# The mixing norms' sums of squares: two 512-column products with a matrix of ones, and each partition's token read from the diagonals

## The chip, the cores and the metric

The kernel runs on one core of one Trainium2 chip. The metric is the device time of one execution in microseconds (us), the median of three runs. Engines are named as in the profile: PE is TensorE's matmul stream, DVE is VectorE, ACT is ScalarE, POOL is GpSimd, SP is the engine that issues most DMAs.

## What is computed

Two layers of an encoder trunk on 512 tokens of 1024 channels. Both halves of a layer begin with an RMS norm: the mixing half (gates, a convolution, three kinds of attention) and the feed-forward half.

```python
def _rmsnorm(x, g):
    xf = x.astype(jnp.float32)
    y = xf * lax.rsqrt(jnp.mean(jnp.square(xf), axis=-1, keepdims=True) + EPS)
    return (y * g.astype(jnp.float32)).astype(x.dtype)

for l in range(DEPTH):
    h = _rmsnorm(x, g_mix[l])
    proj = h @ w_in[l]
    ...
    x = x + mixed @ w_out[l]
    x = x + _conv_ffn(_rmsnorm(x, g_ffn[l]), w_up[l], ...)
```

The kernel multiplies by the gain at once and by the reciprocal root only behind the products, since it is one number per token.

## The kernel before, in words

The stream x lies channel-major: eight tiles of 128 channels by 512 tokens. `norm_tile` (L290 on) writes each tile's gain-scaled copy as two parts that add up to it (`xh`, `xl`, type fp32r) and adds its squares into `sqacc`, 128 by 512, so that the sum over partitions is still to be made. Weights come in units of 128 by 1024: an SP DMA into `w_raw` (L218, two buffers), ACT's high part `w_hi` (L222) and DVE's low part `w_lo` (L224), three buffers each. Every product is then three fp32r matmuls (high by high, low by high, high by low).

Token-major projections (`token_major`, L467 to L469) put 128 tokens on the partitions and 512 output columns in each of four PSUM banks; there the norm is one number per partition, `rstd[:, b]`. Each layer begins with two of them: queries and keys of the neighbourhood attention, into the four banks named aux, and the values (`project_v`), into the four banks named mm. Other projections are channel-major and need the norm as a row `RB`, the same on all partitions.

`finish_norm` makes both for the two mixing norms. It is a generator in the list `side`; `tick` advances it behind a stretch of products, so PE has its matmuls in the middle of the first token-major projection (layer 1) or at its end (layer 0). It makes four matmuls with 128 columns of `sqacc` as weights and one column of ones as the moving operand (L350), which leaves token p of block b in row p, column b of a bank. DVE reads 128 by 4 (L354), takes the reciprocal root by Newton's steps (`newton`, L272 to L277, eleven small operations), and POOL writes `rstd` to DRAM (L358) and reads it back onto all partitions (L362); ACT puts it in the order of the tokens (`RB`, L366). The feed-forward norms (`broadcast_norm`) do it another way: `sqacc` is split into two fp32r parts (`sqh`, `sql`), and two matmuls with a 128 by 128 matrix of ones (L328) leave every token's sum on all partitions.

What follows `rstd` at a layer's start, in the order of the chain: ACT copies the four aux banks to `Q` times `rstd` (L600) and squares them (L501), DVE sums the squares per head (L502), `rsqrt8` takes the root (L575 to L580, with L515 twelve small operations), DVE scales the four `Q` (L519), and PE transposes them by matmuls with an identity (L537), eight at the first visit. PE's own order is fixed: these eight stand behind 72 matmuls of the values' projection.

The order of the work on each engine is made by a scheduler that goes by dependencies and priorities; `self.first()` and the weights' `high_priority` move work ahead, and a smaller edit can move neighbours.

Of the kernel before, what the change touches and what calls it, by code (L numbers as in the profile page):

```python
# [14 lines left out]
F32 = mybir.dt.float32  # L15
F32R = mybir.dt.float32r
I32 = mybir.dt.int32
AF = mybir.ActivationFunctionType
ALU = mybir.AluOpType
# [3 lines left out]
P = 128  # L23
L = 2
D = 1024
S = 512
KT = D // P
NB = S // P
# [6 lines left out]
EPS = 1e-6  # L35
# [16 lines left out]
C_ID, C_ONE, C_COS, C_SIN, C_DIL, C_SWA = 0, 128, 136, 200, 264, 1160  # L52
# [136 lines left out]
class Trunk:  # L189
# [99 lines left out]
    def norm_tile(self, d, xn, pool, lead=False):  # L289
# [17 lines left out]
        else:  # L307
            sq = pool.tile([P, S], F32, name="sq", tag=self.sq_tag, bufs=2)
            nc.scalar.activation(sq, xn, AF.Square)
            nc.vector.tensor_tensor(self.sqacc, self.sqacc, sq, ALU.add)  # L310

    def broadcast_norm(self):

        nc = self.nc
        v = nc.vector
        sqacc = self.sqacc

        def work():
            tile = lambda n, t, dt: self.fp.tile([P, S], dt, name=n, tag=t, bufs=1)
            one, hi, lo = (tile(n, t, F32R) for n, t in (("one", "e0"), ("sqh", "e1"), ("sql", "e2")))  # L320
            v.memset(one[:, :P].bitcast(F32), 1.0)
            with self.first():
                nc.scalar.activation(hi, sqacc, AF.Copy)
                v.tensor_tensor(lo, sqacc, hi.bitcast(F32), ALU.subtract)
            yield
            ps = self.aux()
            for x in (hi, lo):
                nc.tensor.matmul(ps, lhsT=one[:, :P], rhs=x, start=x is hi, stop=x is lo)  # L328
            ms, q = (tile(n, t, F32) for n, t in (("ms", "e3"), ("rs_q", "e5")))
            self.RB = self.norm.tile([P, S + PHASE], F32, name="RB", tag="RB", bufs=1)[:, :S]  # L330
            with self.first():
                v.tensor_scalar(ms, ps, 1.0 / D, EPS, ALU.mult, ALU.add)
                self.newton(ms, tile("rs_i", "e4", I32), q, self.RB)
            yield

        self.side.append(work())

    def finish_norm(self, delay, later=0, mid=0):

        nc = self.nc  # L340
        sqacc = self.sqacc
        self.rstd = self.norm.tile([P, NB], F32, name="rstd", tag="rstd", bufs=2)
        rstd = self.rstd

        def work():
            for _ in range(delay):
                yield
            ps = self.mm()
            for b in range(NB):
                nc.tensor.matmul(ps[:, b:b + 1], lhsT=sqacc[:, b * P:(b + 1) * P],  # L350
                                 rhs=self.cst[:, C_ONE:C_ONE + 1], start=True, stop=True)
            with self.first():
                v = self.norm.tile([P, NB], F32, name="ms", tag="ms", bufs=2)
                nc.vector.tensor_scalar(v, ps[:, 0:NB], 1.0 / D, EPS, ALU.mult, ALU.add)  # L354
                self.rsqrt(self.norm, v, [P, NB], rstd)

            row = self.dram.tile([S], F32, name="row", tag="row", bufs=2)
            nc.gpsimd.dma_start(row.rearrange("(p b) -> p b", p=P), rstd)  # L358
            for _ in range(mid):
                yield  # L360
            raw = self.scratch()
            nc.gpsimd.dma_start(raw, row.unsqueeze(0).broadcast_to([P, S]))  # L362
            for _ in range(later):
                yield
            self.RB = self.norm.tile([P, S + PHASE], F32, name="RB", tag="RB", bufs=1)[:, :S]
            nc.scalar.activation(self.RB.rearrange("q (b p) -> q b p", b=NB),  # L366
                                 raw.rearrange("q (p b) -> q b p", b=NB), AF.Copy)
            yield

        self.side.append(work())  # L370


# [522 lines left out]
    def ffn(self, l, last):  # L895
# [3 lines left out]
        for i in range(4):  # L899
# [3 lines left out]
            U.append(u)  # L903
        F, self.got = [], {}
        self.load_quad(l, 0)
        for i in range(NF):
# [29 lines left out]
            v.tensor_tensor(fl, f, ys[0], ALU.mult)  # L936
            F.append(fl)
            if i in EARLY:
                self.split_pair(F, EARLY.index(i), self.got)
        return F  # L940

# [67 lines left out]

    def split_pair(self, F, j, got):  # L1010

        nc = self.nc
        v = nc.vector
        fi, fk = F[2 * j:2 * j + 2]

# [199 lines left out]
    def layer(self, l):  # L1215
        tc = self.tc
        last = l == L - 1
        self.Y, self.mixed, self.MH, self.glu_u = [None] * 4, [], [], []
        with tc.tile_pool(name="gate", bufs=1, reuse_waits="tile") as self.gp:
            with tc.tile_pool(name="attn", bufs=1, reuse_waits="tile") as self.ap:  # L1220
                self.scratch = lambda: self.gp.tile([P, S], F32, name="raw", tag="t1", bufs=2)
                pss = self.token_major(None, self.aux) if l == 0 else self.early
                Q = self.new_Q()
                for b in range(NB):
                    self.evac_q(Q)(b, pss[b])
                with self.first():
                    for _ in self.qk_stats(Q, 4, 4, None):
                        pass
                self.derive_params()
                V = self.new_V()  # L1230
                self.tabs = [None] * 4
                self.queue(chain(self.na_biases(l, 3 if l else 5), self.qk_norm(Q, 4, 4, 0),
                                 self.attention('na', V, 1)))
                Vd = self.new_V()
                self.project_v(V, Vd)
                Q = self.project_qk()
                ready = self.beside(self.qk_stats(Q, 4, 4, 0))
                self.queue(chain(ready, self.qk_norm(Q, 4, 4, 2), self.attention('dil', Vd, 2)))
                self.glu()
                self.side.append(self.conv())  # L1240
                V = self.new_V()
                Q = self.project_swa(V)
                ready = self.beside(self.qk_stats(Q, 4, 2, 2))
                self.queue(chain(ready, self.qk_norm(Q, 4, 2, 4), self.attention('swa', V, 3)))
                for n in ORDER[:3]:
                    self.gates(n)
                while self.side:
                    self.tick()
            with tc.tile_pool(name="outp", bufs=1, reuse_waits="tile") as self.op:
                self.gates(ORDER[3])  # L1250
                self.xnew = self.new_res()
                self.start_norm('g_ffn')
                for d in range(0, KT, 2):

                    cuts = (0, KT - 2, KT) if d == 0 else (0, KT)
                    pss, ws = [self.mm(), self.mm()], []
                    for k0, k1 in zip(cuts, cuts[1:]):
                        for e in range(2):
                            if k0 == 0:
                                ws.append(self.unit())  # L1260
                            hi, lo = ws[e]
                            for k in range(k0, k1):
                                s = slice(k * P, (k + 1) * P)
                                self.prod(pss[e], hi[:, s], lo[:, s], self.MH[k][0], self.MH[k][1], k == 0,
                                          k == KT - 1)
                            if k1 == KT:
                                self.update(d + e, pss[e], self.op)
                self.xres = self.xnew
                self.broadcast_norm()
        if last:  # L1270
            self.resT = self.dram.tile([S, D], F32, name="resT", tag="resT", bufs=1)
        with tc.tile_pool(name="ffn", bufs=1, reuse_waits="tile") as self.fp:
            self.scratch = lambda: self.fp.tile([P, S], F32, name="raw", tag="cy0", bufs=2)
            F = self.ffn(l, last)
            if last:
                self.down(F, True)
                return
            self.load_prm(l + 1)
            self.xnew = self.new_res()
            self.sq_tag = "fth"  # L1280
            self.start_norm('g_mix')
            self.down(F, False)
            self.finish_norm(5, 8, 4)

            self.early = self.token_major(None, self.aux)
            self.xres = self.xnew
            self.sq_tag = "sq"
# [45 lines left out]
```

## Time and profile before

| | |
|---|---|
| median of 3 runs | 1559.35 us (1559.13 to 1559.58) |
| the profiled execution, its own time | 1559.35 us |
| its span, first to last instruction | 1557.6 us |
| PE busy | 1551.4 us, 7186 instructions |
| DVE busy | 1229.7 us |
| ACT busy | 835.4 us |
[...]

The profiled execution is the median run itself; 1.75 us lie outside its span. A matmul's row is 0.39 us long though the next begins 0.23 us later, because matmuls are pipelined: for PE the distance between starts counts. DVE's and ACT's rows overlap in the same way by less than 0.1 us. The last column of a timeline row, in brackets, is the engine's idle time before it and what ended that.

### The profile page before, as it was taken

The page shows a single profiled execution, that of the slowest core. Times are in us where ns is not written, and L with a number is a line of the kernel's source. Part 1 is how long each engine was busy: PE and PEld are TensorE (multiplying, and loading weights), DVE is VectorE, ACT ScalarE, POOL GpSimd, SP SyncE. Part 2 cuts the span into 40 slices and gives each one's busy share as a digit, 9 for nine tenths or more (in the row PEclk, how much of TensorE's full clock was granted, in tenths as well). Part 3 has the DMA queues.
Part 4 walks back from the last instruction along what each step waited for, and adds up shares of the span by engine and source line. Part 5 has one row for each costly group of instructions (what it writes and reads, how often), then busy time and mean ns, then how long its engine had stood idle before and what let it go on. Part 6 is the DMA issues. An engine that isn't in the chain of part 4 may idle for free.

```text
span 1557.6 us, 20456 instructions
## 1 busy us (share of the span) xinstructions
PE 1551.4 (100%) x7186; PEld 1291.4 (83%) x7186; DVE 1229.7 (79%) x2086; ACT 835.4 (54%) x1420; POOL 175.0 (11%) x304
## 2 busy tenths in 40 slices
PE   9999999999999999999999999999999999999999
PEld 8888888888888888888888888888888888888887
DVE  6689988765689997796676899887656899987964
ACT  6678767333445443364457787772434444443643
POOL 0102002121001111100001020012120111111000
PEclk9999999999999999999999999999999999999999
DMA  6632222232645555576556322213226667665675
GB/s 235 192 93 82 84 85 82 95 96 94 214 161 206 191 187 184 203 239 210 189 180 186 117 72 87 81 69 109 95 95 211 194 221 224 203 214 191 219 231 166
DMA packets 103383, 244.88 MB, mean 157 GB/s; under 512 B 27504, under 2 KB 29424, under 8 KB 103280
## 3 DMA queue, kind: packets, MB, share of 16 engines
q1 hardware_dynamic: 89392, 196.37, 39.5%
q0 software_dynamic: 13600, 46.67, 8.6%
q8 instruction: 57, 0.93, 0.3%
q10 hardware_dynamic: 288, 0.52, 0.1%
q14 instruction: 46, 0.38, 0.1%
HBM read 202.63 MB, written 35.66 MB: 153 GB/s over the span
## 4 chain that ended last, share of the span: by engine, by line
PE 93%; DVE 3%; ACT 3%; issue 0%; DMA 0%; SPq 0%; ACTq 0%; DVEq 0%
PE mm L243 22%; PE mm L245 22%; PE mm L244 22%; PE aux L1052 3%; PE aux L1053 3%; PE aux L1051 3%; PE mm L467 2%; PE mm L469 2%; PE mm L468 2%; PE mm L1052 2%; PE mm L1053 2%; PE mm L1051 2%; PE aux L737 2%; PE aux L699 1%; PE aux L700 1%; PE aux L469 1%
## 5 line engine op out<-in xcount | busy, mean ns | idle before, releaser
L222 ACT ACTIVATE w_hi<-w_raw 128x1024 fp32r<-128x1024 f32 (+1 forms) x305 | 318.7, 1045 | 374.5 <-PE mm L244 203.0
L243 PE MATMUL mm<-xh,w_hi 128*128 128x512 f32 x1280 | 499.6, 390 | 0.0
L245 PE MATMUL mm<-xh,w_lo 128*128 128x512 f32 x1280 | 498.7, 390 | 0.0
L244 PE MATMUL mm<-xl,w_hi 128*128 128x512 f32 x1280 | 498.6, 390 | 0.0
L224 DVE TENSOR_TENSOR w_lo<-w_raw,w_hi 128x1024 fp32r<-128x1024 f32 (+1 forms) x305 | 368.8, 1210 | 81.6 <-ACT w_hi L222 78.0
L245 PEld LDWEIGHTS mm<-xh,w_lo 128*128 128x128 f32 x1280 | 240.3, 188 | 50.7
L243 PEld LDWEIGHTS mm<-xh,w_hi 128*128 128x128 f32 x1280 | 240.3, 188 | 48.9
L244 PEld LDWEIGHTS mm<-xl,w_hi 128*128 128x128 f32 x1280 | 240.4, 188 | 48.7
L841 POOL TENSOR_TENSOR mx<-mx,t 128x512 f32<-128x512 f32 x44 | 66.9, 1528 | 428.7 <-DVE t L840 327.4
L405 DVE SCALAR_TENSOR_TENSOR cv<-cv,prm 128x512 f32<-128x512 f32 x120 | 93.7, 781 | 0.7
L923 ACT ACTIVATE cy<-U,prm 128x512 f32<-128x512 f32 x88 | 70.7, 807 | 35.6 <-DVE U L920 35.4
L920 DVE TENSOR_TENSOR U<-mm,RB 128x512 f32<-128x512 f32 x88 | 60.1, 686 | 33.4 <-PE mm L245 33.3
L811 DVE TENSOR_TENSOR t<-mm,RB 128x512 f32<-128x512 f32 x64 | 44.0, 688 | 47.8 <-PE mm L245 47.4
L467 PE MATMUL mm<-w_hi,xh 128*128 128x512 f32 x192 | 76.4, 398 | 0.4 <-DVE V L595 0.4
L468 PE MATMUL mm<-w_lo,xh 128*128 128x512 f32 x192 | 75.0, 390 | 0.0
L469 PE MATMUL mm<-w_hi,xl 128*128 128x512 f32 x192 | 74.8, 390 | 0.0
L724 ACT ACTIVATE e<-e,rl 128x256 f32<-128x256 f32 (+2 forms) x96 | 57.4, 598 | 23.3 <-DVE rl L723 23.1
L925 DVE SCALAR_TENSOR_TENSOR cy<-U,prm,cy 128x512 f32<-128x512 f32 x88 | 65.5, 746 | 1.3
L924 DVE SCALAR_TENSOR_TENSOR cy<-U,prm,cy 128x512 f32<-128x512 f32 x88 | 65.3, 744 | 0.6 <-ACT cy L923 0.6
L989 POOL DMA_DIRECT2D sums<-t x44 | 24.0, 544 | 342.0 <-DVE t L983 314.0
L929 ACT ACTIVATE fth<-cy 128x512 f32<-128x512 f32 x44 | 27.8, 632 | 63.8 <-DVE cy L925 63.7
L717 ACT ACTIVATE e<-e,nm 128x256 f32<-128x256 f32 (+2 forms) x96 | 57.6, 600 | 2.7
(304 smaller groups left out, 2625.9 us busy)
## 6 DMA issues: line engine op xcount, KB each, us to landing
w_raw<-W SPq DMA_DIRECT2D x223, 512.0 KB, 3.6
quad<-W POOLq DMA_DIRECT2D x44, 512.0 KB, 5.4
w_raw<-W SPq DMA_DIRECT2D x66, 256.0 KB, 3.7
sums<-t POOLq DMA_DIRECT2D x44, 256.0 KB, 3.0
sums<-quad POOLq DMA_DIRECT2D x44, 256.0 KB, 3.8
w_raw<-sums SPq DMA_DIRECT2D x44, 256.0 KB, 3.6
w_raw<-sums SPq DMA_DIRECT2D x22, 512.0 KB, 4.8
res<-xn SPq DMA_DIRECT2D x24, 256.0 KB, 2.5
```

What stands on the lines that cost most here:

```text
L222: w = nc.scalar.activation(hi[:, s], raw[:, s], AF.Copy)
L224: nc.vector.tensor_tensor(lo[:, s], raw[:, s], hi[:, s].bitcast(F32), ALU.subtract)
L243: mm(ps, lhsT=wh, rhs=xh, start=start, stop=False)
L244: mm(ps, lhsT=wh, rhs=xl, start=False, stop=False)
L245: self.last_mm = mm(ps, lhsT=wl, rhs=xh, start=False, stop=stop)
L405: self.after_mm(v.scalar_tensor_tensor(acc, u[:, t:t + S], w(t), acc, ALU.mult, ALU.add))
L467: mm(pss[b], lhsT=self.Xh[k][:, t], rhs=hi[:, s], start=k == 0, stop=False)
L468: mm(pss[b], lhsT=self.Xh[k][:, t], rhs=lo[:, s], start=False, stop=False)
L469: self.last_mm = mm(pss[b], lhsT=self.Xl[k][:, t], rhs=hi[:, s], start=False, stop=k == KT - 1)
L1051: mm(ps, lhsT=x[0], rhs=w[0][:, cols], start=start, stop=False, skip_group_check=again)
L1052: mm(ps, lhsT=x[0], rhs=w[1][:, cols], start=False, stop=False, skip_group_check=again)
L1053: self.last_mm = mm(ps, lhsT=x[1], rhs=w[0][:, cols], start=False, stop=stop, skip_group_check=again)
```

## The change

`sum_squares` is new and serves both kinds of norm. For the mixing norms the four one-column matmuls become the two of the feed-forward norms: `sqacc` is split by ACT and DVE into `sqh` and `sql`, and PE makes two products of 512 columns with ones. Every partition of the bank then holds all 512 sums. DVE reads from it, per block of 128 columns, the element on the diagonal: a `tensor_tensor_reduce` with the identity matrix, which multiplies, scales by 1/1024 and adds up from EPS into `ms[:, b]`. Each is two instructions on DVE, the operation (128 by 128) and the reading of its accumulator (128 by 1). The split is emitted one tick ahead of the products, the products at the tick where the matmuls were. `rstd`, the row in DRAM and `RB` are made as before. The feed-forward norms' instructions stay.

```diff
+    def sum_squares(self, tile):
+        nc = self.nc
+        one, hi, lo = (tile(n) for n in ("one", "sqh", "sql"))
+        nc.vector.memset(one[:, :P].bitcast(F32), 1.0)
+        with self.first():
+            nc.scalar.activation(hi, self.sqacc, AF.Copy)
+            nc.vector.tensor_tensor(lo, self.sqacc, hi.bitcast(F32), ALU.subtract)
+
+        def products(ps):
             for x in (hi, lo):
                 nc.tensor.matmul(ps, lhsT=one[:, :P], rhs=x, start=x is hi, stop=x is lo)
+            return ps
+        return products
...
     def finish_norm(self, delay, later=0, mid=0):
...
-            for _ in range(delay):
+            for _ in range(delay - 1):
                 yield
-            ps = self.mm()
-            for b in range(NB):
-                nc.tensor.matmul(ps[:, b:b + 1], lhsT=sqacc[:, b * P:(b + 1) * P],
-                                 rhs=self.cst[:, C_ONE:C_ONE + 1], start=True, stop=True)
+            products = self.sum_squares(self.ones_tile)
+            yield
+            ps = products(self.mm())
             with self.first():
-                v = self.norm.tile([P, NB], F32, name="ms", tag="ms", bufs=2)
-                nc.vector.tensor_scalar(v, ps[:, 0:NB], 1.0 / D, EPS, ALU.mult, ALU.add)
-                self.rsqrt(self.norm, v, [P, NB], rstd)
+                ms = self.norm.tile([P, NB], F32, name="ms", tag="ms", bufs=2)
+                junk = self.scratch()
+                for b in range(NB):
+                    s = slice(b * P, (b + 1) * P)
+                    nc.vector.tensor_tensor_reduce(out=junk[:, s], in0=ps[:, s], in1=self.ident, scale=1.0 / D,
+                                                   scalar=EPS, op0=ALU.mult, op1=ALU.add, accum_out=ms[:, b:b + 1])
+                self.rsqrt(self.norm, ms, [P, NB], rstd)
...
+                self.ones_tile = lambda n: self.ap.tile([P, P if n == "one" else S], F32R, name=n, tag=n, bufs=1)
...
+            self.ones_tile = lambda n: self.fp.tile([P, S], F32R, name=n,
+                                                    tag={"one": "e0", "sqh": "t3", "sql": "t2"}[n], bufs=1)
```

The scheduler also moves three neighbours. Lines below L345 stand ten further down in the change (L578 before is L588).

On DVE at the first mixing norm, before: the read of the sums, then Newton's steps with a weight split (`w_lo_445`) between them.

```order
L224 TENSOR_TENSOR w_lo_415<-w_raw_413,w_hi_414 128x1024
L354 TENSOR_SCALAR ms_322<-mm_317 128x4
L272 TENSOR_SCALAR rs_i_324<-ms_322 128x4
L273 TENSOR_SCALAR rstd_197<-rs_i_324 128x4
L275 SCALAR_TENSOR_TENSOR rs_q_325<-rstd_197 128x4
L276 TENSOR_TENSOR rs_q_325<-rs_q_325,ms_322 128x4
L277 SCALAR_TENSOR_TENSOR rstd_197<-rs_q_325,rstd_197 128x4
L224 TENSOR_TENSOR w_lo_445<-w_raw_443,w_hi_444 128x1024
```

The same place in the change, where the pair of L363 stands four times in a row (once here), and the same weight split is now `w_lo_453`.

```order
L224 TENSOR_TENSOR w_lo_423<-w_raw_421,w_hi_422 128x1024
L363 ISA raw_327,ms_326<-mm_323,cst_72 128x128
L363 ISA ms_326 128x1
...
L224 TENSOR_TENSOR w_lo_453<-w_raw_451,w_hi_452 128x1024
L272 TENSOR_SCALAR rs_i_332<-ms_326 128x4
L273 TENSOR_SCALAR rstd_197<-rs_i_332 128x4
```

The weight split moved from the middle of Newton's steps to their front; it stays ahead of `rstd`. The second mixing norm reads alike.

On DVE a little later, the end of `rsqrt8` and the scaling of the four `Q` in layer 0, before: two weight splits stand behind the scaling.

```order
L578 SCALAR_TENSOR_TENSOR r8_q_364<-r8_y_363 128x4x8
L579 TENSOR_TENSOR r8_q_364<-r8_q_364,ss_349 128x4x8
L580 SCALAR_TENSOR_TENSOR r8_y_363<-r8_q_364,r8_y_363 128x32
L519 TENSOR_TENSOR Q_341<-Q_341,r8_y_363 128x512
...
L519 TENSOR_TENSOR Q_344<-Q_344,r8_y_363 128x512
L224 TENSOR_TENSOR w_lo_548<-w_raw_546,w_hi_547 128x1024
L224 TENSOR_TENSOR w_lo_635<-w_raw_633,w_hi_634 128x1024
```

The same place in the change:

```order
L588 SCALAR_TENSOR_TENSOR r8_q_372<-r8_y_371 128x4x8
L224 TENSOR_TENSOR w_lo_556<-w_raw_554,w_hi_555 128x1024
L589 TENSOR_TENSOR r8_q_372<-r8_q_372,ss_357 128x4x8
L590 SCALAR_TENSOR_TENSOR r8_y_371<-r8_q_372,r8_y_371 128x32
L529 TENSOR_TENSOR Q_349<-Q_349,r8_y_371 128x512
...
L529 TENSOR_TENSOR Q_352<-Q_352,r8_y_371 128x512
L224 TENSOR_TENSOR w_lo_643<-w_raw_641,w_hi_642 128x1024
```

One weight split (`w_lo_548` before, `w_lo_556` now) moved from behind the scaling of the queries and keys to two operations ahead of it, in layer 0 and in layer 1.

On SP at layer 1's start, the loads of the neighbourhood attention's bias tables (L639 and L640, from TB) among those of the weights, before:

```order
L888 DMA res7_6491<-xn_7510 128x512
L639 DMA mx_7777<-TB 128x256
L640 DMA mx_7773<-TB 128x512
L218 DMA w_raw_7743<-W 128x1024
L639 DMA mx_7777<-TB 128x256
L640 DMA mx_7774<-TB 128x512
L639 DMA tab_7778<-TB 128x256
L640 DMA mx_7775<-TB 128x512
L639 DMA tab_7778<-TB 128x256
L640 DMA mx_7776<-TB 128x512
L218 DMA w_raw_7816<-W 128x1024
```

The same place in the change:

```order
L898 DMA res7_6499<-xn_7518 128x512
L218 DMA w_raw_7759<-W 128x1024
L649 DMA mx_7793<-TB 128x256
L650 DMA mx_7789<-TB 128x512
L218 DMA w_raw_7832<-W 128x1024
L649 DMA mx_7793<-TB 128x256
L650 DMA mx_7790<-TB 128x512
L649 DMA tab_7794<-TB 128x256
L650 DMA mx_7791<-TB 128x512
L649 DMA tab_7794<-TB 128x256
L650 DMA mx_7792<-TB 128x512
```

Each of the two weight loads moved ahead by a group of table loads: `w_raw_7816` stood behind all eight, and `w_raw_7832` now stands ahead of the last six.

## Rows read from the trace of the kernel before

**Rows 1.** The page, part 1: engines' busy time over the span.

```profile
PE 1551.4 (100%) x7186; PEld 1291.4 (83%) x7186; DVE 1229.7 (79%) x2086; ACT 835.4 (54%) x1420; POOL 175.0 (11%) x304
```

**Rows 2.** PE's waits over the span: engine line, releaser: total, times, longest.

```profile
PE mm L467 <- DVE V L595: 0.4, 1, 0.4
```

**Rows 3.** PE's timeline at layer 0's norm, 20 to 34 us: start, length, instruction.

```profile
19.67 0.39 PE L468 MATMUL aux<-w_lo,xh 128*128 128x512 f32 x1
...
27.61 0.95 PE L350 MATMUL mm<-cst,sqacc 128*128 128x1 f32 x8
28.42 0.49 PE L467 MATMUL mm<-w_hi,xh 128*128 128x512 f32 x1
...
31.05 0.39 PE L469 MATMUL mm<-w_hi,xl 128*128 128x512 f32 x1
```

**Rows 4.** PE's timeline at layer 1's norm, 788 to 806 us.

```profile
798.30 0.95 PE L350 MATMUL mm<-cst,sqacc 128*128 128x1 f32 x8
```

**Rows 5.** Timeline at layer 0's feed-forward norm, 436 to 446 us.

```profile
439.25 0.39 PE L328 MATMUL aux<-sqh,one 128*128 128x512 f32 x1
...
439.47 0.39 PE L328 MATMUL aux<-sql,one 128*128 128x512 f32 x1
...
439.90 0.69 DVE L332 TENSOR_SCALAR ms<-aux 128x512 f32<-128x512 f32 x1 [1.15 <-PE aux L328]
```

**Rows 6.** PE's timeline at the first transposes of Q, layer 0 and layer 1.

```profile
44.89 1.03 PE L537 MATMUL aux<-cst,Q 128*128 128x128 f32 x8
...
815.58 1.03 PE L537 MATMUL aux<-cst,Q 128*128 128x128 f32 x8
```

**Rows 7.** DVE's timeline in layer 0, from the sums to the scaled Q.

```profile
28.59 0.16 DVE L354 TENSOR_SCALAR ms<-mm 128x4 f32<-128x4 f32 x1 [3.91 <-PE mm L350]
28.79 0.17 DVE L272 TENSOR_SCALAR rs_i<-ms 128x4 int32<-128x4 int32 x1
...
29.67 1.22 DVE L224 TENSOR_TENSOR w_lo<-w_raw,w_hi 128x1024 fp32r<-128x1024 f32 x1
30.81 0.15 DVE L275 SCALAR_TENSOR_TENSOR rs_q<-rstd 128x4 f32<-128x4 f32 x1
...
38.33 0.18 DVE L515 TENSOR_SCALAR ss<-ss 128x32 f32<-128x32 f32 x1
...
41.01 2.49 DVE L519 TENSOR_TENSOR Q<-Q,r_y 128x512 f32<-128x512 f32 x4
```

**Rows 8.** DVE's timeline in layer 1, the scaled Q.

```profile
811.78 2.50 DVE L519 TENSOR_TENSOR Q<-Q,r_y 128x512 f32<-128x512 f32 x4
```

**Rows 9.** ACT's timeline in layer 0, from rstd to the next weights.

```profile
31.99 1.27 ACT L600 ACTIVATE Q<-aux,rstd 128x512 f32<-128x512 f32 x2 [3.12 <-DVE rstd L277]
...
38.76 1.12 ACT L366 ACTIVATE RB<-raw 128x512 f32<-128x512 f32 x1 [1.19 <-DMA raw<-row]
39.78 1.05 ACT L222 ACTIVATE w_hi<-w_raw 128x1024 fp32r<-128x1024 f32 x1
```

**Rows 10.** ACT's timeline in layer 1, RB.

```profile
809.20 1.12 ACT L366 ACTIVATE RB<-raw 128x512 f32<-128x512 f32 x1 [0.86 <-DMA raw<-row]
```

**Rows 11.** DVE's timeline in the attention: operations with an accumulator.

```profile
88.63 0.40 DVE L713 CUSTOM_DVE_ANT_0 e<-aux,tab 128x256 f32<-128x256 f32 x1
88.96 0.08 DVE L713 DVE_READ_ACCUMULATOR2_ANT mx<- 128x1 f32 x1
...
126.25 0.68 DVE L713 CUSTOM_DVE_ANT_0 e<-aux,tab 128x512 f32<-128x512 f32 x1
```

**Rows 12.** SP's and POOL's timeline at layer 1's start: DMA issues, first start and spread.

```profile
795.50 0.33 SPq L218 DMA_DIRECT2D w_raw<-W  x1
...
801.62 14.14 SPq L218 DMA_DIRECT2D w_raw<-W  x3
...
802.95 0.54 POOL L358 DMA_DIRECT2D row<-rstd  x1 [8.33 <-DVE rstd L277]
```

**Rows 13.** Line L640, the wide bias tables' eight loads: issue to landing.

```profile
DMA to landing us min/median/max: 2.7/4.6/5.8
```

More of the change, by code (lines that the diff above doesn't have):

```diff
@@ L310, in norm_tile, with broadcast_norm, work @@
             nc.vector.tensor_tensor(self.sqacc, self.sqacc, sq, ALU.add)
-    def broadcast_norm(self):
+    def sum_squares(self, tile):
         nc = self.nc
[L315 to L326, printed above, removed]
+        one, hi, lo = (tile(n) for n in ("one", "sqh", "sql"))
[4 more added lines that the diff above has]
+        def products(ps):
             for x in (hi, lo):
                 nc.tensor.matmul(ps, lhsT=one[:, :P], rhs=x, start=x is hi, stop=x is lo)
-            ms, q = (tile(n, t, F32) for n, t in (("ms", "e3"), ("rs_q", "e5")))
+            return ps
+        return products
+    def broadcast_norm(self):
+        v = self.nc.vector
+        def work():
+            tile = lambda n, t, dt=F32: self.fp.tile([P, S], dt, name=n, tag=t, bufs=1)
+            products = self.sum_squares(lambda n: tile(n, {"one": "e0", "sqh": "e1", "sql": "e2"}[n], F32R))
+            yield
+            ps = products(self.aux())
+            ms, q = tile("ms", "e3"), tile("rs_q", "e5")
             self.RB = self.norm.tile([P, S + PHASE], F32, name="RB", tag="RB", bufs=1)[:, :S]
@@ L340, in finish_norm @@
         nc = self.nc
-        sqacc = self.sqacc
         self.rstd = self.norm.tile([P, NB], F32, name="rstd", tag="rstd", bufs=2)
@@ L345, in work @@
         def work():
-            for _ in range(delay):
+            for _ in range(delay - 1):
                 yield
-            ps = self.mm()
-            for b in range(NB):
-                nc.tensor.matmul(ps[:, b:b + 1], lhsT=sqacc[:, b * P:(b + 1) * P],
-                                 rhs=self.cst[:, C_ONE:C_ONE + 1], start=True, stop=True)
+            products = self.sum_squares(self.ones_tile)
+            yield
+            ps = products(self.mm())
             with self.first():
-                v = self.norm.tile([P, NB], F32, name="ms", tag="ms", bufs=2)
-                nc.vector.tensor_scalar(v, ps[:, 0:NB], 1.0 / D, EPS, ALU.mult, ALU.add)
-                self.rsqrt(self.norm, v, [P, NB], rstd)
+                ms = self.norm.tile([P, NB], F32, name="ms", tag="ms", bufs=2)
[5 more added lines that the diff above has]
+                self.rsqrt(self.norm, ms, [P, NB], rstd)
             row = self.dram.tile([S], F32, name="row", tag="row", bufs=2)
```

## The prediction, made before the changed kernel ran

> **What bounds the kernel now.** I read the page first, then PE's waits, then the timelines around the two mixing norms. PE is busy for 1551.4 of 1557.6 us [rows 1]; what the other engines do matters only where PE arrives and something isn't there. In PE's list of waits the only one near the mixing norms is 0.4 us for a bank of the values' projection [rows 2], and none stands at the transposes of `Q`. So the change has two sides: what it takes off PE's own stream, and whether the chain from the sums to the scaled `Q`, which it lengthens, still ends before PE's eight transposes. The rows to look at for the second are where PE reaches them (44.89 and 815.58, [rows 6]) and when DVE has scaled the last `Q`: 41.01 + 2.49 = 43.50 in layer 0 [rows 7] and 811.78 + 2.50 = 814.28 in layer 1 [rows 8]. The fourth of the eight transposes is the first that reads the last `Q`, some 0.3 us behind the first. The slack before is thus about 45.2 - 43.5 = 1.7 us in layer 0 and 815.9 - 814.3 = 1.6 us in layer 1.
>
> **PE's own stream.** Between 19.67 and 27.61 lie 35 matmuls, so one takes 7.94/35 = 0.227 us; the norm's matmuls, eight records in a row, take 28.42 - 27.61 = 0.81; and from 28.42 to 31.05 eleven matmuls take 2.63 where 11 x 0.227 = 2.49 are their pace, so 0.14 more is lost behind the one-column matmuls [rows 3]. That is 0.95 us. The two products that come instead go at the usual pace: the feed-forward norm's two start 439.47 - 439.25 = 0.22 apart [rows 5], 0.45 for both. Gain 0.95 - 0.45 = 0.50 us; layer 1 has the same group of the same length [rows 4], so **-1.0 us in all**.
>
> **The split.** `sqh` on ACT, `sql` and the memset on DVE come a tick earlier than the products, in stretches in which both engines idle: DVE had waited 3.91 us for PE at the sums [rows 7]. I cost them at nothing. If that cover were gone, PE would wait for `sql` at the second product, up to ACT's and DVE's two operations of some 0.7 us each; the feed-forward norm, which does the same, shows no PE wait. The bank: in layer 0 the fourth bank of the values' projection is now freed by four reads, not one; PE asks for it nine matmuls on, 28.07 + 2.04 = 30.1, and the reads end near 29.3 (below), so nothing.
>
> **From the sums to rstd.** In the feed-forward norm DVE starts 439.90 - 439.47 = 0.43 us behind the start of the second product [rows 5]. Here that product starts at 27.61 + 0.23 = 27.84, so DVE starts at 28.27, 0.32 earlier than at 28.59 [rows 7]. The single read, 28.79 - 28.59 = 0.20, is replaced by four pairs, of a kind that no row has at 128 columns. The nearest rows are the attention's: 0.40 us at 256 columns and 0.68 at 512 [rows 11], so 0.14 less per 128 columns: 0.26 long at 128. The accumulator's read starts 0.33 us behind its operation at 256 columns, 0.19 at 128 by the same slope. Below, a pair costs those 0.19; above, 0.26 and the read's own 0.08, 0.34 in all. I take 0.25, between them, since DVE's rows overlap a little. The weight split (30.81 - 29.67 = 1.14, [rows 7]) stood ahead of the end of Newton's steps and still does, so its move costs nothing here. `rstd` comes later by 4 x 0.25 - 0.20 - 0.32 = **0.5 us** (0.2 to 0.8).
>
> [...]
>
> **From rstd to the scaled Q.** Layer 0: the row goes through DRAM to `RB` and the next `w_hi` stands behind `RB` on ACT (38.76, then 39.78 with 1.05, so it ends at 40.83, [rows 9]). Both follow `rstd`: `w_hi` ends at 41.3. ACT's copies and squares of `Q` start with `rstd` at 31.99 [rows 9]; among them only the order of one `w_hi` changes. DVE's twelve small operations, 38.33 to 41.01 or 0.223 each [rows 7], start at 38.8; ten of them are done at 41.05. Then comes the weight split that now stands there. It waits for `w_hi` until 41.3 and takes 1.14, the last two operations 0.45, and the scaling starts at 42.9, 1.9 us later than before. The last `Q` is ready at 43.50 + 1.9 = 45.4, and PE wants it at 45.2 - 0.5 = 44.7. **PE waits 0.8 us**, counting a little for the semaphore. Behind that wait stands PE's whole queue; nothing that follows makes it up, since PE has next to no waits to lose.
>
> Layer 1: `RB` at 809.20 [rows 10] becomes 809.7, `w_hi` ends some 2.1 later at 811.8, the split and two operations take 1.6, and the scaling starts at 813.4 for 811.78: 1.6 later. The last `Q` is ready at 815.9, PE wants it at 815.4: 0.6 with the semaphore, if the DMAs take what they took.
>
> **SP's queue in layer 1.** They won't quite. The weight load that now stands ahead of the last six table loads waits for a buffer that DVE frees behind the norm; its counterpart was issued at 801.62 [rows 12], while the tables were through before it. So six loads, 1.15 MB, are now issued from about 801.6 on, just as POOL writes `rstd` (802.95, [rows 12], now 803.4). The tables themselves are wanted some 25 us later, so their delay costs nothing. But the write and `RB` can come later, and with them `w_hi`, the split and `Q`. Below: nothing, since the write already shared the DMA engines with a weight load. Above: a table load takes 2.7 us at best and 5.8 at worst [rows 13], so 3.1 us. I take 0.6, near the lower end, because the write is small and the load at 801.62 was beside it before too. Layer 1 waits 0.6 + 0.6 = **1.2 us**.
>
> **Sum.** -1.0 + 0.8 + 1.2 = +1.0 us on the profiled execution's 1559.35, which is also the median of the runs: **1560.4 us**. A measurement of this kernel can tell about 0.2%, 3.1 us, from no change, so this is no difference that can be seen: between 1556.2 and 1562.5.
>
> **Rivals.**
> - The wait isn't there. The scaling would have to end less than 1.2 us later than now (1.7 of slack less 0.5). For it: the pair may cost 0.19, and `w_hi` may not bind. Against: the weight split alone is 1.14 us of it and `rstd` is later besides. Then only PE's gain is left: 1558.4. Chance 0.14.
> - The four pairs at their full length, operation and read one after the other, 0.34 or more: `rstd` is later by another 0.4 us or so, and both waits with it: 1561.2. [...] Against: DVE's rows overlap elsewhere (the split of 29.67 ends at 30.89, the next starts at 30.81, [rows 7]). [...] Chance 0.18.
> - Slower, by the DMAs: the row and `RB` of layer 1 are held behind the tables by the full 3.1 us of [rows 13]. Then `w_hi`, the split and the scaling come 3.1 us later, PE waits 3.7 in layer 1 instead of 1.2, and the time is 1559.35 - 1.0 + 0.8 + 3.7 = 1562.9. It decides from the point where SP's six loads are all queued before POOL's write, which is nearly so; against it speaks the write's small size. Chance 0.14, of which 0.10 lies beyond 1562.5.
> - PE gets no gain, because the two products start late or at another pace; the feed-forward norm's rows speak against it. Since the `Q` decide when PE goes on, PE would arrive 0.5 us later at each place and wait 0.5 us less there: about 1560.4 again, to be told from the forecast by the rows alone. Chance 0.04.
>
> **How the numbers follow.** The forecast has a chance of 0.50 and its own range, 1559.3 to 1561.6, comes from 0.19 and 0.34 for the pair and from 0 to 1.2 for the DMAs. The range of 8 in 10 reaches to most of the first rival and to the lower part of the third: 1558.8 to 1562.4. Faster by over 0.2% would need a gain of three times PE's: 0.02. Slower by over 0.2%: 0.10. Within: 0.88.
>
> **What would show it.** Two matmuls of 0.227 us at the norms and none of the 0.14 lost behind them; DVE's four pairs near 28.3 with 0.25 from pair to pair; `rstd` read by ACT at 32.5; the first transposes stretched from 0.8 to about 1.6 us in layer 0 and to 2 us in layer 1, with a PE wait on DVE's `Q`. In layer 1 `RB` some 1 us later than 809.2. The prediction is wrong if PE's waits show no new entry on `Q`, if a wait appears elsewhere, such as at the values' banks or the first scores, or if the median lies outside 1556.2 to 1562.5.

## The result, and the profile after

The changed kernel takes **1563.88 us** (median of ten runs, 1562.37 to 1564.50) against 1559.52 for the kernel before (ten runs, 1559.13 to 1559.77): a ratio of 1.0026 with a 95% interval of 1.0018 to 1.0034. It is slower by 4.4 us. The forecast was 1560.4 with a range up to 1562.4, so the time lies above the range. The profiled execution took 1563.89, its span is 1562.1; that is 4.54 and 4.5 more than the profiled execution of before, so the rows below can be set beside the rows of before.

The page's first part, of the changed kernel:

```profile
PE 1553.4 (99%) x7174; PEld 1291.9 (83%) x7174; DVE 1232.9 (79%) x2104; ACT 836.0 (54%) x1422; POOL 174.9 (11%) x304
```

PE has twelve records fewer than in [rows 1] and yet is busy 2.0 us longer, which fewer matmuls alone can't give. PE's waits show where most of the rest is; the columns are as in [rows 2]:

```profile
PE aux L547 <- DVE Q L529: 2.9, 5, 1.7
```

PE's timeline at layer 0's norm, at the first transposes of `Q` in layer 0, and from there in layer 1 to the second transposes (L547 is L537 of before):

```profile
27.80 0.39 PE L323 MATMUL mm<-sqh,one 128*128 128x512 f32 x1
28.02 0.39 PE L323 MATMUL mm<-sql,one 128*128 128x512 f32 x1
28.25 0.39 PE L477 MATMUL mm<-w_hi,xh 128*128 128x512 f32 x1
...
44.58 0.56 PE L547 MATMUL aux<-cst,Q 128*128 128x128 f32 x3
45.44 0.74 PE L547 MATMUL aux<-cst,Q 128*128 128x128 f32 x5 [0.30 <-DVE Q L529]
45.93 0.48 PE L477 MATMUL mm<-w_hi,xh 128*128 128x512 f32 x1
...
814.86 0.39 PE L479 MATMUL mm<-w_hi,xl 128*128 128x512 f32 x1
816.93 0.30 PE L547 MATMUL aux<-cst,Q 128*128 128x128 f32 x1 [1.68 <-DVE Q L529]
817.53 0.30 PE L547 MATMUL aux<-cst,Q 128*128 128x128 f32 x1 [0.30 <-DVE Q L529]
818.13 0.30 PE L547 MATMUL aux<-cst,Q 128*128 128x128 f32 x1 [0.30 <-DVE Q L529]
818.73 0.75 PE L547 MATMUL aux<-cst,Q 128*128 128x128 f32 x5 [0.30 <-DVE Q L529]
819.22 0.69 PE L477 MATMUL mm<-w_hi,xh 128*128 128x512 f32 x1
819.71 0.63 PE L478 MATMUL mm<-w_lo,xh 128*128 128x512 f32 x1
820.14 0.63 PE L479 MATMUL mm<-w_hi,xl 128*128 128x512 f32 x1
...
823.65 1.03 PE L547 MATMUL aux<-cst,Q 128*128 128x128 f32 x8
```

The same places in the kernel before, behind [rows 6]:

```profile
45.68 0.48 PE L467 MATMUL mm<-w_hi,xh 128*128 128x512 f32 x1
...
816.37 0.48 PE L467 MATMUL mm<-w_hi,xh 128*128 128x512 f32 x1
...
819.19 1.03 PE L537 MATMUL aux<-cst,Q 128*128 128x128 f32 x8
```

Four readings, from the first row on:
- The two products start 0.22 apart and the next matmul 0.23 behind: 0.45 for both, nothing lost behind them. The gain of 0.50 per norm is there.
- Layer 0: from the start of the transposes to the next matmul PE takes 45.93 - 44.58 = 1.35, before 45.68 - 44.89 = 0.79. **Wait 0.56.**
- Layer 1: the matmul ahead of the transposes starts at 814.86, so that PE, at 0.23 from start to start, arrives at 815.09. It goes on at 819.22, 4.13 later; before it took 816.37 - 815.58 = 0.79. **Wait 3.34**, a stop before each of the first four transposes. (The brackets count from the end of a row and come to less.)
- Behind that wait the matmuls are 0.43 apart instead of 0.23. From the next matmul to the second transposes it takes 823.65 - 819.22 = 4.43, before 819.19 - 816.37 = 2.82. **1.61 more**, without any wait.

The sum -1.0 + 0.56 + 3.34 + 1.61 = 4.51 is the 4.5 us by which the spans differ. The last term is TensorE's clock; the granted clock, as a share of its full level, is the column behind POOL's, then DMA share and GB/s:

```profile
core 0: us, PE busy (x) PEld busy (x) DVE busy (x) ACT busy (x) POOL busy (x), PEclk, DMA share, GB/s
...
820.00:822.00 2.00, 2.00 (x6) 1.54 (x6) 1.91 (x4) 1.67 (x3) 0.00 (x0) 0.50 0.45 94
822.00:824.00 2.00, 2.00 (x11) 1.58 (x10) 0.70 (x2) 0.00 (x0) 0.00 (x0) 0.82 0.90 303
```

And in the kernel before:

```profile
820.00:822.00 2.00, 2.00 (x12) 1.68 (x10) 1.97 (x4) 1.65 (x4) 0.00 (x0) 1.00 1.01 324
```

Behind the waits the granted clock stands at 0.50 of its full level, and it comes back within the stretch that begins at 822 (0.82); in the kernel before it is 1.00 in both stretches. The ten executions of the changed kernel fit this: the shortest, of 1562.37, has a mean clock of 1.000, the others 0.998 or 0.999 (0.999 also occurs in the kernel before, whose profiled execution has 1.000).

Why is `Q` so late in layer 1? The chain read backwards, DVE's timeline first, from the pairs on:

```profile
798.97 0.29 DVE L363 CUSTOM_DVE_ANT_0 raw<-mm,cst 128x128 f32<-128x128 f32 x1 [2.83 <-PE mm L323]
799.18 0.08 DVE L363 DVE_READ_ACCUMULATOR2_ANT ms<- 128x1 f32 x1
...
799.82 1.22 DVE L224 TENSOR_TENSOR w_lo<-w_raw,w_hi 128x1024 fp32r<-128x1024 f32 x1
...
814.50 1.23 DVE L224 TENSOR_TENSOR w_lo<-w_raw,w_hi 128x1024 fp32r<-128x1024 f32 x1 [2.84 <-ACT w_hi L222]
...
816.09 2.50 DVE L529 TENSOR_TENSOR Q<-Q,r_y 128x512 f32<-128x512 f32 x4
```

The four pairs take 799.82 - 798.97 = 0.85, 0.21 each. The accumulator's read, 0.08 long, adds nothing: the second pair's operation starts with the first pair's read, at 799.18. So it was in the kernel before, where an operation starts together with the read of [rows 11]:

```profile
88.96 0.42 DVE L745 TENSOR_TENSOR pt<-aux,pt 128x256 fp32r<-128x256 f32 x1
```

Later DVE stands 2.84 us at the weight split of 814.50, two small operations short of the scaling. ACT's timeline shows what it waits for:

```profile
812.41 1.11 ACT L376 ACTIVATE RB<-raw 128x512 f32<-128x512 f32 x1 [3.78 <-DMA raw<-row]
813.43 1.04 ACT L222 ACTIVATE w_hi<-w_raw 128x1024 fp32r<-128x1024 f32 x1
```

`RB` is 3.21 us later than in [rows 10]. POOL's and SP's timelines tell why:

```profile
803.39 0.54 POOL L368 DMA_DIRECT2D row<-rstd  x1 [8.71 <-DVE rstd L277]
808.47 0.54 POOL L372 DMA_DIRECT2D raw<-row  x1 [4.55 <-DMA row<-rstd]
```
```profile
801.07 0.33 SPq L218 DMA_DIRECT2D w_raw<-W  x1
801.45 0.42 SPq L649 DMA_DIRECT2D mx<-TB  x1
...
803.81 0.43 SPq L650 DMA_DIRECT2D mx<-TB  x1
```

And POOL's timeline of the kernel before:

```profile
805.77 0.54 POOL L362 DMA_DIRECT2D raw<-row  x1 [2.28 <-DMA row<-rstd]
```

The write of `rstd` is issued in the middle of six table loads and holds POOL for 4.55 us; before, it held POOL for 2.28.

The tables didn't become late by the scheduler's choice alone. In SP's waits of the changed kernel one wide table load stands for PE's products:

```profile
SPq L650 <- PE mm L323: 2.6, 1, 2.6
```

The split's tiles of layer 1 lie where tables are to go, so SP stops there until the products have read them. The kernel before has no such wait at this place.

### The profile page after: what moved, and what is told of

It reads as the page before. It is cut to its first block, busy times and chain, and to the rows that moved or that the text cites. A ratio compares the mean times of both kernels' runs of the same rounds, so it can differ in the third digit from the quotient of the medians.

```text
span 1562.1 us, 20450 instructions
## 1 busy us (share of the span) xinstructions
PE 1553.4 (99%) x7174; PEld 1291.9 (83%) x7174; DVE 1232.9 (79%) x2104; ACT 836.0 (54%) x1422; POOL 174.9 (11%) x304
## 4 chain that ended last, share of the span: by engine, by line
PE 90%; DVE 3%; issue 3%; ACT 3%; DMA 1%; POOL 0%; ACTq 0%; POOLq 0%; DVEq 0%
PE mm L243 21%; PE mm L245 21%; PE mm L244 21%; PE aux L1063 3%; PE aux L1062 3%; PE aux L1061 3%; PE mm L1063 2%; PE mm L1062 2%; PE mm L1061 2%; PE mm L477 2%; PE mm L478 2%; PE mm L479 2%; PE aux L747 2%; PE aux L709 1%; PE aux L710 1%
```

## The experiments

The theory after these rows: the loss is not the norm's arithmetic. Two moves in the order make it together, the tables ahead of the row and the split ahead of the scaling, and the wait that they make costs clock as well. Each experiment moves one thing. The moves are made by a dependency that only the scheduler sees, or by a priority. The first experiment (and with it the one that undoes both) also puts the split's tiles of layer 1 elsewhere, which takes away the tables' wait for PE's products. Times stand beside the runs of the kernel before on the same chip: median 1559.47 for the first four, 1559.54 for the next four (33 runs each).

### Tables early again

```diff
-            self.nc.sync.dma_start(m, self.TB[l, h][:, 0:256])
-            self.nc.sync.dma_start(ends[h], self.TB[l, h][:, 256:768])
+            with self.tc.high_priority(offset=3100) if l else nullcontext():
+                self.nc.sync.dma_start(m, self.TB[l, h][:, 0:256])
+                self.nc.sync.dma_start(ends[h], self.TB[l, h][:, 256:768])
...
-                                                    tag={"one": "e0", "sqh": "t3", "sql": "t2"}[n], bufs=1)
+                                                    tag={"one": "fh20", "sqh": "fh18", "sql": "fh19"}[n], bufs=1)
```

> The changed kernel with layer 1's eight table loads issued ahead of the second weight load again, as they stand before the change (the norm's three tiles are put where no table buffer lies over them, and the loads get a higher priority). The place of the weight split stays where the change put it. Theory (the late tables hold the row of rstd, and with it RB, w_hi, the split and Q): the row takes some 2.3 us again, RB comes near 809.7 instead of 812.41, the scaling of Q starts near 813.4 instead of 816.09, PE waits under 0.6 us at the first transposes of layer 1, no matmuls at half clock behind them, time near 1559.5 (1559.0 to 1560.5). Rival (the four pairs and the split's place are the cost, the tables are beside it): PE's wait stays at 2 us or more and the time at 1563 to 1564.

Measured: 1560.31 (ratio 1.0006, 0.9997 to 1.0015). ACT's and DVE's timelines in layer 1:

```profile
810.23 1.11 ACT L377 ACTIVATE RB<-raw 128x512 f32<-128x512 f32 x1 [1.82 <-DMA raw<-row]
```
```profile
812.32 1.22 DVE L225 TENSOR_TENSOR w_lo<-w_raw,w_hi 128x1024 fp32r<-128x1024 f32 x1 [0.89 <-ACT w_hi L223]
```

With the tables early 3.5 of the 4.4 us are gone. `RB` didn't quite come back: the row still held POOL for 2.62 us, and PE still waits 0.81 us in three stops in layer 1 (0.21 and two of 0.30), where under 0.6 was expected. The clock stayed at 1.00.

### The weights' w_hi ahead of RB on ACT

```diff
-            nc.scalar.activation(self.RB.rearrange("q (b p) -> q b p", b=NB),
-                                 raw.rearrange("q (p b) -> q b p", b=NB), AF.Copy)
+            c = nc.scalar.activation(self.RB.rearrange("q (b p) -> q b p", b=NB),
+                                     raw.rearrange("q (p b) -> q b p", b=NB), AF.Copy)
+            u = self.nn and len(self.w_list) // L + 7
...
+            if u in self.his:
...
+                self.tc.add_manual_dep(c.ins, self.his[u].ins.name, info, reason="pace")
```

(`self.his` holds the `w_hi` of the weights.)

> The changed kernel with one pair of ScalarE's instructions in layer 1 swapped: the w_hi that the split in the middle of the Newton steps waits for goes ahead of RB. Tables and row stay late. Theory (the split holds the scaling only because its w_hi stands behind RB, and RB behind the late row): RB still near 812.4 or later, w_lo near 811.5 instead of 814.50, scaling near 813.3 instead of 816.09, PE waits under 0.6 us in layer 1, no half clock, time near 1559.5 (1559.0 to 1560.5). Rival (the late row or the crowded DMA engines cost by themselves, wherever w_hi stands): 1562 or more.

Measured: 1559.43 (1.0000, 0.9991 to 1.0009). ACT and DVE in layer 1:

```profile
809.73 1.06 ACT L222 ACTIVATE w_hi<-w_raw 128x1024 fp32r<-128x1024 f32 x1 [1.22 <-PE mm L485]
811.75 1.14 ACT L377 ACTIVATE RB<-raw 128x512 f32<-128x512 f32 x1 [0.97 <-DMA raw<-row]
```
```profile
811.46 1.22 DVE L225 TENSOR_TENSOR w_lo<-w_raw,w_hi 128x1024 fp32r<-128x1024 f32 x1
```

The row is nearly as late as in the changed kernel (POOL held for 4.33 us, `RB` at 811.75 for 812.41), and no loss is left in the times, because nothing that PE needs soon stands behind it any more. One swap of two instructions takes back the whole 4.4 us.

### The split behind the scaling

```diff
-                    nc.vector.tensor_tensor(lo[:, s], raw[:, s], hi[:, s].bitcast(F32), ALU.subtract)
+                    w = nc.vector.tensor_tensor(lo[:, s], raw[:, s], hi[:, s].bitcast(F32), ALU.subtract)
+                    if self.w_emitted in (8, len(self.w_list) // L + 7):
...
+                        self.tc.add_manual_dep(w.ins, self.scaled.ins.name, info, reason="pace")
```

(`self.scaled` is the last of the four scalings of `Q`.)

> The changed kernel with, in both layers, the weight split that stands in the middle of the Newton steps moved behind the scaling of Q, where it stands before the change. Tables, row and RB stay late. Theory (everything is lost through that split): the scaling starts near 41.7 in layer 0 and near 812.1 in layer 1, no PE wait at the first transposes of either layer, no half clock, the gain of 1.0 us of PE's own stream is kept: 1558.4 (1557.9 to 1559.1). Rival (the four pairs make rstd late, and that is the cost): still 1561 or more. Second rival (the split is then late for PE): PE waits on w_lo somewhere behind, 1559.5 or more.

Measured: 1558.53 (0.9996, 0.9987 to 1.0005). PE and DVE in layer 1:

```profile
814.68 1.03 PE L550 MATMUL aux<-cst,Q 128*128 128x128 f32 x8
```
```profile
811.73 2.50 DVE L532 TENSOR_TENSOR Q<-Q,r_y 128x512 f32<-128x512 f32 x4
```

No wait at the transposes of either layer. The median is 0.94 below that of before, the gain forecast for PE's own stream; the interval of the ratio holds 1, so that this kernel beats the one before is not shown by the times.

### PE kept busy during the wait

```diff
             ps = self.aux()
+            for _ in range(self.fill):
+                nc.tensor.matmul(ps, lhsT=self.Xh[0][:, :P], rhs=self.Xh[0], start=True, stop=True)
+            self.fill = 0
```

(`self.fill` is 10 at the start of layer 1, 0 in layer 0.)

> The changed kernel with ten 512-column matmuls (2.3 us at PE's pace) ahead of the first transposes of layer 1, into the bank that the transposes then overwrite: nothing is computed with them, they only keep PE busy while Q is late. Theory (of the 4.5 us that the changed kernel loses up to the second transposes of layer 1, some 1.6 are not the wait but matmuls at half clock behind it, because PE idled): the first transposes still end near 819.2, the granted clock stays at 1.00 behind them, and the time is 1562.2 (1561.7 to 1562.7). Rival (the half clock has nothing to do with PE's idle time): matmuls 0.43 apart all the same, 1563.9. Rival (the whole loss is the wait): clock full, time still 1563.5 to 1564.5.

Measured: 1562.31 (1.0018, 1.0008 to 1.0027). PE around the transposes, DVE's scaling, and the clock behind them:

```profile
815.91 2.43 PE L547 MATMUL aux<-xh 128*128 128x512 f32 x10
818.18 0.43 PE L550 MATMUL aux<-cst,Q 128*128 128x128 f32 x2
...
819.52 0.74 PE L550 MATMUL aux<-cst,Q 128*128 128x128 f32 x5 [0.30 <-DVE Q L529]
...
822.85 1.03 PE L550 MATMUL aux<-cst,Q 128*128 128x128 f32 x8
```
```profile
816.88 2.50 DVE L529 TENSOR_TENSOR Q<-Q,r_y 128x512 f32<-128x512 f32 x4
```
```profile
820.00:822.00 2.00, 2.00 (x12) 1.67 (x11) 1.91 (x3) 1.76 (x3) 0.00 (x0) 1.00 0.23 41
```

From the fourth stop to the second transposes it is 822.85 - 819.52 = 3.33 us, in the changed kernel 823.65 - 818.73 = 4.92. `Q` is as late as there: PE came to this place 0.82 behind (815.91 for 815.09; this profiled execution took 1563.0), and the scaling began 0.79 behind (816.88 for 816.09). The fillers run while `Q` is missing, and two of the stops of 0.30 remain. Yet the median is 2.84 above the kernel before instead of 4.36, with ten matmuls more. So some 1.5 us of the loss are clock, an estimate from the two medians (4.36 - 2.84), and with PE at work during the wait the clock was 1.00 in the stretch in which the changed kernel has 0.50.

### Each move alone in the kernel before, and both

Late tables (the last six loads held behind the second weight load):

```diff
+            with self.tc.high_priority(offset=3100) if l and h else nullcontext():
...
+                if l and h:
...
+                    self.tc.add_manual_dep(d.ins, self.los[len(self.w_list) // L + 6].ins.name, info, reason="pace")
```

> The kernel before with nothing but the last six table loads of layer 1 held behind the second weight load on SP, as they stand in the changed kernel. The norm is the old one and the weight split stands behind the scaling of Q. Theory (late tables cost nothing unless the split stands ahead of the scaling): the row of rstd lands 2 us later, RB and the w_hi behind it too, but the scaling stays near 811.8, PE waits nowhere new: 1559.5 (1559.1 to 1559.9). Rival (the late row, RB or the crowded DMA engines cost by themselves): 1561 or more.

Early split (`self.los` holds the weight splits, `self.r8` is the last multiplication of the Newton steps):

```diff
+                    if self.w_emitted in (8, len(self.w_list) // L + 7):
...
+                        self.tc.add_manual_dep(self.r8.ins, self.los[self.w_emitted].ins.name, info, reason="pace")
```

> The kernel before with nothing but the weight split held ahead of the last two Newton steps, where the changed kernel has it, in both layers. Tables and norm are the old ones. Theory (the split in that place costs only what the slack of 1.7 and 1.6 us doesn't hold): the scaling starts near 42.4 instead of 41.01 in layer 0 and near 812.9 instead of 811.78 in layer 1, PE waits 0.1 us at most: 1559.5 (1559.2 to 1560.0). Rival (the split's place alone makes the wait): 1561 or more.

Both together:

> The kernel before with both of these: late tables and the split ahead of the last two Newton steps. The norm is the old one: four one-column matmuls, no pairs. Theory (these two together are the loss, the norm's new operations only 0.4 us of it): scaling near 815.6 in layer 1, PE waits about 0.7 us and three times 0.3 at the first transposes, 2.4 us in all by the last of them, and what half clock follows comes on top: 1561.8 without, 1563.4 with 1.6 us of half clock. Rival (the pairs or the products are the loss): 1559.5.

Measured: late tables 1559.49 (1.0000, 0.9991 to 1.0009), although the write of `rstd` held POOL for 3.89 us in it. Early split 1559.85 (1.0001, 0.9992 to 1.0010). Both 1563.34 (1.0025, 1.0016 to 1.0034). Neither move alone is seen in the times. Both together cost 3.80 of the 4.36 that the changed kernel loses, in a kernel that has neither the new products nor the pairs. That settles the main cause. The other half microsecond is near the 0.44 by which the new norm makes `rstd` later; no run moved that alone.

### Both undone in the changed kernel

The diffs of the first and the third experiment together.

> The changed kernel with the tables early and the split behind the scaling: the new norm alone. Theory (each of the two suffices in layer 1, but only the split's place helps in layer 0): no PE wait at the first transposes, 1.0 us less than the kernel before, as with the split alone: 1558.5 (1558.0 to 1559.0). Rival (the late row cost something that the split behind the scaling did not undo): 1558 or less.

Measured: 1558.52 (0.9994, 0.9985 to 1.0003), as the theory has it: beyond the split's place, early tables bring nothing more that the times can show.

### The same waits with and without half clock

The kernel with both moves had spread from 1561.39 to 1566.16, so it was profiled twice more.

> The kernel before with late tables and early split once more, for a second profile: its times spread from 1561.4 to 1566.2, and the first profile, of an execution of 1561.93, shows PE's waits of 0.99 and three times 0.30 without any half clock. Theory (the spread is half clock behind those waits, in some executions and not in others): a profiled execution of 1563 or more shows the same waits and a granted clock near 0.5 for 2 to 4 us behind them; one under 1562.7 shows a clock of 1.00 there. Rival (the spread is in the waits or elsewhere): a slow execution with the clock at 1.00 behind the transposes.

> The same kernel a third time, with the same expectation: half clock behind the transposes of layer 1 where the profiled execution takes 1563 or more, none where it takes less than 1562.7.

Measured: 1563.64 and 1561.50, one execution each, beside 1559.78 for the kernel before. PE of the first of the two, then its clock:

```profile
816.65 0.30 PE L542 MATMUL aux<-cst,Q 128*128 128x128 f32 x1 [0.54 <-DVE Q L524]
...
818.46 0.74 PE L542 MATMUL aux<-cst,Q 128*128 128x128 f32 x5 [0.30 <-DVE Q L524]
...
823.37 1.03 PE L542 MATMUL aux<-cst,Q 128*128 128x128 f32 x8
```
```profile
820.00:822.00 2.00, 2.00 (x6) 1.52 (x6) 1.91 (x4) 1.39 (x3) 0.00 (x0) 0.50 0.54 123
```

And of the earlier profile of the same kernel, an execution of 1561.93:

```profile
816.61 0.30 PE L542 MATMUL aux<-cst,Q 128*128 128x128 f32 x1 [0.99 <-DVE Q L524]
...
818.41 0.74 PE L542 MATMUL aux<-cst,Q 128*128 128x128 f32 x5 [0.30 <-DVE Q L524]
...
821.73 1.03 PE L542 MATMUL aux<-cst,Q 128*128 128x128 f32 x8
```
```profile
820.00:822.00 2.00, 2.00 (x12) 1.64 (x11) 1.91 (x4) 1.34 (x3) 0.00 (x0) 1.00 0.67 141
```

From the fourth stop to the second transposes: 4.91 us at half clock, 3.32 without; the execution of 1561.50 shows 3.35 and a clock of 1.00. The one that lost the clock had the shorter first wait of these two. So in one of three profiled executions of this kernel the clock fell to 0.50 behind the waits, and in two it stayed at 1.00; what decides it stays open. Half clock is also not the whole spread, as the theory had it: of the first eleven executions the one of 1563.34 shows a mean clock of 1.000, and the one of 1566.16 lies 2.5 us above the profiled one at half clock. Where their time went is not known.

## Why the prediction was wrong

Its chain to PE was right. In layer 1 one term of the sum was far too small, the wait of the row of `rstd` at the DMAs, and one was missing, the clock. Either alone would have left the time inside the range, which ends at 1562.4: 1559.35 - 1.0 + 0.56 + 3.34 = 1562.25 with the longer wait alone, 1560.4 + 1.61 = 1562.0 with the clock alone. Together they put it beyond. In the order of its steps:

- **PE's own stream, -1.0 us: right.** Two products in 0.45, nothing lost behind them. With the split back in its place the medians are 0.94 and 1.02 below, though both intervals hold 1.
- **The pair, 0.25 us: nearly right.** 0.21 from pair to pair, 0.85 for four, since the accumulator's read, 0.08 long, starts together with the next operation and costs nothing of its own on the path. The trace of before showed that already, in the row behind the read of [rows 11]. In layer 1 `row` was issued at 803.39 for 802.95, 0.44 later, where the prediction had 0.5. An operation's row is 0.28 to 0.29 long, but the next starts 0.21 behind it.
- **Layer 0, a wait of 0.8: right in kind, 0.56 in size.** The scaling began at 42.79 (42.9 forecast).
- **Layer 1's DMA term, 0.6 us: the first step that failed.** "I take 0.6, near the lower end, because the write is small and the load at 801.62 was beside it before too." The six loads were issued at 801.45 to 803.81 and the write at 803.39, as forecast, but POOL was held 4.55 us by it instead of 2.28, and the read of the row landed half a microsecond later as well (812.41 - 808.47 = 3.94 for 809.20 - 805.77 = 3.43). `RB` is 3.21 later, 0.44 of that from `rstd`: the term is **2.77**, near the upper bound of 3.1 and not near the lower. Not all of it is the tables: with them early `RB` came 7.07 and 6.68 us behind the write (in the first experiment and with both undone), before 6.25, so 0.4 to 0.8 of the 2.77 has a cause that stays open.
- **What followed from `RB` was right.** `w_hi` behind it, the split behind `w_hi`, the scaling behind the split, PE behind that: with 2.77 in place of 0.6 the forecast wait of 1.2 becomes 3.4, and 3.34 was measured.
- **The clock: the second step that failed, a term that was missing.** PE's stop was priced as time alone, and nothing was said on what follows it. It cost 1.61 us more of half clock.

The third rival (the row held by the full 3.1 us, PE waits 3.7, 1562.9) is nearly what happened, with the clock on top: without half clock the filler's kernel took 1562.31. Its price was argued away by the size of the write, of which no row spoke; the rows that the prediction shows for such a write are of one with a single load beside it. The second rival, the pairs at full length, fell: they cost 0.21. The first, no wait, fell too. The fourth would have shown in the products' rows and didn't.

## What to carry to other kernels

When a change makes a chain longer by half a microsecond, look less at the operations than at the order that comes out: here a split and six loads changed their places, and neither alone was seen in the times, but one put the scaling behind a DMA and the other put that DMA among 1.15 MB of loads. A new tile can move loads too, when it lies where their data is to go (SP's 2.6 us here). Before pricing an instruction moved into a chain, ask what it waits for itself; a free move turns dear once its own input is late (1559.85 with the split early alone, 1563.34 with the tables late as well). Hold such an instruction where it was, by an ordering dependency: here the median then fell by what the arithmetic promised, 0.94 us, which is too little to be told from noise.

## What the runs showed of the hardware

- PE's granted clock fell to 0.50 behind a wait of 1.68 us and three of 0.30 (as the brackets count), and in another execution already behind 0.54 and three of 0.30; behind 0.99 and three of 0.30 it stayed at 1.00. With ten matmuls ahead of the transposes, and only two stops of 0.30 left, it also stayed at 1.00. What makes it fall, no run shows.
- In layer 1 the write of `rstd`, one row of 512 values (2.0 KB), held POOL for 2.28 us beside one weight load before the change, for 2.24 to 2.62 in the three other kernels that issued it behind the tables, and for 3.59 to 4.55 in the six kernels that issued it among them. The write was the same in all; what differed was the loads issued around it.
